# Order of the matmuls at the end of the output projection, and a PSUM value half copied out at the turn from up- to down-projection

## The chip, the cores and the metric

The kernel runs on one core of one Trainium2 chip. The metric is the device time of one execution in microseconds (us); lower is better. Three executions of the kernel before took 933.41, 936.21 and 936.86 us; their median, 936.21 us, is the number that the changed kernel is compared with.

## What is computed

One layer of a diffusion backbone for 512 latent tokens of width 1024, in float32. The last two parts matter here: the token mixer's output projection with its residual, and the feed-forward part with a 3x3 depthwise convolution (the tokens are an image of 8 rows and 64 columns).

```python
def _conv_ffn(h, rows, w_up, conv_w, conv_b, w_down):
    a, val = _split(h @ w_up, (D_FF, D_FF))                 # D_FF = 2816
    img = a.reshape(bsz, rows, length // rows, D_FF)
    a = conv3x3_depthwise(img, conv_w) + conv_b
    return (gelu(a) * val) @ w_down
...
x = x + g1x * (merged @ w_o)
hx2 = _modulate(_rms_norm(x, norm2_g), sh2x, sc2x)
x = x + g2x * _conv_ffn(hx2, rows, w_up, conv_w, conv_b, w_down)
return _rms_norm(x, final_norm_g)
```

## The kernel before

**Three matmuls for one.** Every float32 operand is split in a high part (rounded to the matmul's input type) and a low part (the rest). ScalarE (ACT) casts the high part, VectorE (DVE) subtracts to get the low part, and TensorE (PE) runs three matmuls: high by high, high by low, low by high. In the names, wh and wl are the parts of weights, h2h and h2l those of the normalised input of the feed-forward part, eh, el, sh, sl those of activations of the down-projection.

**Who sets the order.** The kernel is written with a tile framework: each engine's instructions are put in an order by the framework's scheduler from the written program, its own costs and the data dependencies, and every engine then runs its own list strictly in that order. The helper in_order (lines 81 to 90) chains all instructions of one engine from a given point, so that the scheduler keeps the written order there. DMA loads are issued from SyncE's queue (SP); some weight tiles get a second operand added by an accumulating DMA from GpSimd's queue (POOL).

**Output projection** (strassen, lines 445 to 494, called at 1494). The 512x1024 by 1024x1024 product is done in seven half-size products (Strassen-Winograd); each is 24 matmuls per pair of weight loads, done in two steps of 12 (j = 0, 1). Four PSUM banks of the pool "gl" and four of the pool "mm" hold the sums. The last product, s4, adds to the pair of gl banks c and completes the quarter for tokens 0 to 255. wo_done (1476 to 1487) is called for each finished 128x512 piece: DVE multiplies by the gate and adds to the residual x1, ACT squares for the norm. When a token row's two halves are there, norm2_tok makes its scale and the scaled tile xs on ACT. norm2_part (1453 to 1470) then transposes xs on PE into a gl bank, ACT turns each 128x256 piece into h2h and h2f (scale and shift), and DVE makes h2l. The tokens 256 to 511 are finished before s4 starts, so their transposes can be done while s4 runs: they stand in the list todo, whose entries are taken one at each step of the product (wo_step).

**Up-projection** (1530 to 1536, 1646 to 1658). It starts with four column blocks at once (prods_cm, line 388), whose matmuls for tokens 256 to 511 need h2h and h2l of one k after the other, k = 0 to 7. Then 20 more blocks f follow, each with two products of 24 matmuls into two mm banks: pa, which goes through the convolution, and pv, the value half. conv_part (1512 to 1528) copies pa out (ca), starts the accumulator (cacc) on ACT, adds eight taps on DVE (line 1523), applies gelu on ACT (1524), and multiplies by pv straight from its PSUM bank on DVE (1525). Every second block ends with four DVE sums, token_sums.

**Down-projection** (1538 to 1792). Again Strassen-Winograd, over 11 pairs p of hidden blocks. Units "x" (one p, 12 matmuls, banks p1 and p5, gl pool), "t3" and "t2" (two p each, 12 matmuls, banks p7 and p6, mm pool) alternate: x0, x1, t3, t2, x2, x3, t3, t2, and so on. prep(i) issues the work that unit i needs: for x (x_prep, 1572) an in-place add on the freshly loaded raw tile (line 1578, DVE), its split (ACT cast, DVE subtract, 1567 and 1568), splits of the activations (374, 375) and the sum t (1582, DVE); for t3 and t2 two half-tile splits. prep runs two units ahead of the matmuls (LEAD = 2). Weight pairs wh, wl rotate through five buffers, raw tiles through four.

At the turn, in the last up block f = 21, the first loads and the first two units are prepared, then conv_part for f = 21 is written, and then the loop over units starts. The mm pool has four banks: p7 takes two that are free, and the second p6 bank is the one in which pv of f = 21 lies.

## Time and profile before

| | |
|---|---|
| median of three executions | 936.21 us (933.41 to 936.86) |
| the profiled execution | 938.85 us, of which the span from first to last instruction is 937.1 us |
| mean granted TensorE clock | 0.990 |
| PE busy | 906.9 us, 97% of the span |
| DVE busy | 755.3 us, 81% |
| ACT busy | 484.2 us, 52% |
| HBM traffic | 142 GB/s over the span |

How to read the profile: times are us from the start of the span. A row of the timeline has the start, the duration, the engine, the line of the kernel, the operation, what it writes and reads, and in brackets how long the engine stood idle before it and what released it. Matmuls overlap, so the time that one costs is the distance between two starts, not the duration. A row of the windows view has the stretch, its length, then for each engine the busy time and the number of instructions, the granted TensorE clock (1.00 is full), the share of the DMA engines that is busy, and GB/s. The chain of waits is followed back from the last instruction: each row names what the end was waiting for at that time.

### The profile page before, as it was taken

The numbers are of one execution on the slowest core, as the hardware profiler recorded it, in microseconds if no ns is written. First come the engines' busy times: TensorE is split into PE (matmuls) and PEld (weight loads), VectorE is DVE, ScalarE is ACT, GpSimd is POOL, SyncE is SP. The second block draws the span as 40 slices with busy tenths as digits, with TensorE's granted clock in tenths as the row PEclk, the third lists the DMA queues.
The fourth block names the chain that finished last, engine by engine and source line by source line (L and its number), as shares of the span: only waits on it lengthen the run. The fifth ranks groups of instructions, "written<-read, shape, count | busy, mean of one in ns | idle before, by whom it ended". The sixth has DMA issues, their size and how long they took to land.

```text
span 937.1 us, 12863 instructions
## 1 busy us (share of the span) xinstructions
PE 906.9 (97%) x4671; PEld 758.9 (81%) x4671; DVE 755.3 (81%) x1312; ACT 484.2 (52%) x871; POOL 62.1 (7%) x90
## 2 busy tenths in 40 slices
PE   6999999999999999999999998999999999989996
PEld 4776898988888888878888877988888888868885
DVE  5567759689589877878776886999988898999797
ACT  5136546557465546656652569533333443356574
POOL 3000000000000011112011010000000000022100
PEclk9999999999999999999999999999999999989999
DMA  9941411141079375968677164344434333499432
GB/s 271 334 131 28 131 46 46 46 113 49 20 229 329 122 195 115 281 153 230 174 194 210 28 176 136 95 142 135 124 116 142 103 90 113 99 248 218 125 108 90
DMA packets 125820, 134.26 MB, mean 143 GB/s; under 512 B 7177, under 2 KB 84309, under 8 KB 125757
## 3 DMA queue, kind: packets, MB, share of 16 engines
q1 hardware_dynamic: 115357, 116.80, 40.1%
q0 software_dynamic: 8672, 15.43, 10.2%
q10 hardware_dynamic: 1728, 1.22, 0.4%
q8 instruction: 37, 0.61, 0.3%
q14 instruction: 26, 0.21, 0.1%
HBM read 131.32 MB, written 2.10 MB: 142 GB/s over the span
## 4 chain that ended last, share of the span: by engine, by line
PE 78%; DVE 10%; DMA 5%; ACT 3%; issue 2%; SPq 1%; ACTq 0%; DVEq 0%
PE mm L382 32%; PE mm L408 9%; PE gl L1625 6%; PE gl L455 5%; PE mm L1625 4%; PE gl L408 3%; PE mm L455 3%; PE gl L904 3%; PE mm L401 3%; DMA raw<-in_w_in_dram 2%; DVE wl L144 1%; PE mm L694 1%; PE mm L1008 1%; DVE bc L872 1%; PE mm L393 1%
## 5 line engine op out<-in xcount | busy, mean ns | idle before, releaser
L143 ACT CAST wh<-raw 128x1024 fp32r<-128x1024 f32 x110 | 115.0, 1049 | 89.0 <-PE mm L382 55.5
L144 DVE TENSOR_TENSOR wl<-raw,wh 128x1024 fp32r<-128x1024 f32 x110 | 133.9, 1220 | 31.3 <-ACT wh L143 30.9
L382 PE MATMUL mm<-h2l,wh 128*128 128x512 f32 (+1 forms) x352 | 133.7, 380 | 0.0
L382 PE MATMUL mm<-h2h,wl 128*128 128x512 f32 (+1 forms) x352 | 133.5, 379 | 0.0
L382 PE MATMUL mm<-h2h,wh 128*128 128x512 f32 (+1 forms) x352 | 133.5, 379 | 0.0
L1523 DVE SCALAR_TENSOR_TENSOR cacc<-ca,ccol,cacc 128x441 f32<-128x441 f32 (+2 forms) x176 | 121.7, 694 | 4.4 <-ACT cacc L1517 0.9
L382 PEld LDWEIGHTS mm<-h2l,wh 128*128 128x128 f32 x352 | 66.2, 188 | 12.6 <-DVE h2l L1470 0.2
L382 PEld LDWEIGHTS mm<-h2h,wl 128*128 128x128 f32 x352 | 66.2, 188 | 12.5
L382 PEld LDWEIGHTS mm<-h2h,wh 128*128 128x128 f32 x352 | 66.2, 188 | 12.5
L1524 ACT ACTIVATE cacc<-cacc 128x512 f32<-128x512 f32 x22 | 13.9, 633 | 91.9 <-DVE cacc L1523 91.9
L1157 DVE SCALAR_TENSOR_TENSOR acc<-wa,cs,acc 128x512 f32<-128x512 f32 x64 | 45.6, 747 | 4.2 <-DMA wa<-in_w_ada_dram 4.2
L382 PE MATMUL mm<-hxh,wh 128*128 128x512 f32 x104 | 41.7, 401 | 0.0
L382 PE MATMUL mm<-hxh,wl 128*128 128x512 f32 x104 | 40.9, 394 | 0.0
L382 PE MATMUL mm<-hxl,wh 128*128 128x512 f32 x104 | 40.7, 392 | 0.0
L218 DVE TENSOR_TENSOR wl<-tt,wh 128x512 fp32r<-128x512 f32 x48 | 31.7, 687 | 9.5 <-ACT wh L217 9.4
L217 ACT CAST wh<-tt 128x512 fp32r<-128x512 f32 x48 | 28.5, 622 | 19.9 <-DMA tt<-in_w_in_dram 7.5
L1567 ACT CAST wh<-raw 128x1024 fp32r<-128x1024 f32 x22 | 23.0, 1052 | 18.9 <-PE mm L1625 6.1
L193 POOL DMA_DIRECT2D tt<-in_w_in_dram x24 | 20.8, 1086 | 167.5 <-DVE xl L1258 72.1
L1568 DVE TENSOR_TENSOR wl<-raw,wh 128x1024 fp32r<-128x1024 f32 x22 | 26.9, 1222 | 4.4 <-ACT wh L1567 4.3
L455 PE MATMUL mm<-wl,hxh 128*128 128x512 f32 x72 | 28.1, 391 | 0.8 <-DVE wl L144 0.8
L455 PE MATMUL mm<-wh,hxh 128*128 128x512 f32 x72 | 28.1, 390 | 0.0
L455 PE MATMUL mm<-wh,hxl 128*128 128x512 f32 x72 | 28.0, 389 | 0.0
(522 smaller groups left out, 2397.5 us busy)
## 6 DMA issues: line engine op xcount, KB each, us to landing
raw<-in_w_in_dram SPq DMA_DIRECT2D x54, 512.0 KB, 4.7
wa<-in_w_ada_dram SPq DMA_DIRECT2D x96, 256.0 KB, 5.4
raw<-in_ffn_w_up_dram SPq DMA_DIRECT2D x44, 512.0 KB, 4.1
raw<-in_ffn_w_down_dram SPq DMA_DIRECT2D x22, 512.0 KB, 3.4
tt<-in_w_in_dram POOLq DMA_DIRECT2D x24, 256.0 KB, 6.7
raw<-in_w_br_a_dram SPq DMA_DIRECT2D x8, 512.0 KB, 5.3
raw<-in_w_br_b_dram SPq DMA_DIRECT2D x8, 512.0 KB, 4.4
raw<-in_w_o_dram SPq DMA_DIRECT2D x8, 512.0 KB, 5.9
```

The source lines that it names most:

```text
L143: A.copy(wh, raw)
L144: V.tensor_tensor(wl, raw, wh.bitcast(F32), op=ALU.subtract)
L217: A.copy(wh[:, kk, :], tt[j][kk])
L218: V.tensor_tensor(wl[:, kk, :], tt[j][kk], wh[:, kk, :].bitcast(F32), op=ALU.subtract)
L382: T.matmul(ps, a[:, k, :], b[:, c0:c0 + n], start=(k == 0 and i == 0), stop=(k == KT - 1 and i == 2))
L401: T.matmul(ps, a[:, t * P:(t + 1) * P], b[:, k % 4, :], start=(k == 0 and i == 0), stop=(k == KT - 1 and i == 2))
L408: T.matmul(ps, a, b[:, k % 2, :], start=(k == 0 and i == 0), stop=(k == KT - 1 and i == 2))
L455: T.matmul(ps[t], a, b[:, kk, :], start=(first and i == 0), stop=(j == 1 and kk == 1 and i == 2), skip_group_check=again)
L904: T.matmul(ps, p_, q_, start=(start and z == 0), stop=(stop and z == 2))
L1157: V.scalar_tensor_tensor(a_, w_, cs[:, k, 0:1], a_, op0=ALU.mult, op1=ALU.add)
L1523: V.scalar_tensor_tensor(o, a_[:, r0 + dy:r1 + dy, c0 + dx:c1 + dx], wcol(tap), o, op0=ALU.mult, op1=ALU.add)
L1625: T.matmul(ps, a[:, t * P:(t + 1) * P], w[b][:, j, c0:c0 + n], start=(first and i == 0), stop=(last and i == 2), skip_group_check=again)
```

## The change

The diff has two parts that don't touch each other.

1. In strassen, for the output projection only (low_first), all PE instructions from the product a12 (in c11) to the end of s4 are chained in written order. The transposes for tokens 256 to 511 move in the written program: instead of two pieces at the two steps of s4, all four come with the second step, after s4's last matmul (three idle entries in todo, then one entry for all).
2. conv_part becomes a generator, conv_steps. For the last block f = 21 its first piece runs where conv_part ran, and copies pv out of its bank into an SBUF tile pvc on ACT. The eight taps follow in pairs, one pair after each of the first down units, and gelu, the product with pvc and the token sums after the fourth pair.

```diff
+        start = len(traced())
         if low_first:
             c11()
         prod(c, "s4", True)
+        if low_first:
+            in_order(start, T.engine)
...
-                todo.extend([idle, idle, lambda: norm2_parts(1, (0, 1)), lambda: norm2_parts(1, (2, 3))])
+                todo.extend([idle] * 3 + [lambda: norm2_parts(1, range(4))])
...
-    def conv_part(f, pa, pv):
+    def conv_steps(f, pa, pv, keep=False):
         wcol = lambda tap: ccol[:, tap * FT + f:tap * FT + f + 1]
         a_ = heap([P, 8, GW], s="ca")
         A.copy(a_, pa)
         acc = heap([P, 8, GW], s="cacc")
         A.activation(acc, pa, AF.Identity, bias=ccol[:, 198 + f:199 + f], scale=wcol(4))
-        for tap in (0, 1, 2, 3, 5, 6, 7, 8):
+        gact.append(acc)
+        if keep:
+            pv_ = heap([P, 512], s="pvc")
+            A.copy(pv_, pv)
+            pv = pv_
+        yield
+        for n_, tap in enumerate((0, 1, 2, 3, 5, 6, 7, 8)):
...
+            if n_ % 2:
+                yield
         A.activation(acc, acc, AF.Gelu)
         V.tensor_tensor(acc, acc, pv.rearrange("p (r w) -> p r w", w=GW), op=ALU.mult)
-        gact.append(acc)
         if f % 2:
             token_sums(f // 2)
+
+    def conv_part(f, pa, pv):
+        for _ in conv_steps(f, pa, pv):
+            pass
...
-        conv_part(f, pa, pv)
+            last_conv = conv_steps(f, pa, pv, True)
+            next(last_conv)
+        else:
+            conv_part(f, pa, pv)
...
     for i in range(NX - 3):
         prep(i + LEAD)
+        next(last_conv, None)
         steps_x(i)
```

How the scheduler's lists change. First PE at the end of the output projection, before. gl_5604 and gl_5605 are the banks c of s4; wh_5720 and wl_5721 are the weights of its second step; rows that read ident are transposes, and xs_5703 and xs_5716 are scaled token tiles.

```order
L455 MATMUL gl_5605<-wh_5676,ml_5415 128x512
L1459 MATMUL gl_5782<-ident,xs_5703 128x128
L1459 MATMUL gl_5794<-ident,xs_5703 128x128
L455 MATMUL gl_5604<-wh_5720,mh_5354 128x512
L1459 MATMUL gl_5782<-ident,xs_5716 128x128
L1459 MATMUL gl_5782<-ident,xs_5703 128x128
L1459 MATMUL gl_5782<-ident,xs_5716 128x128
L1459 MATMUL gl_5794<-ident,xs_5716 128x128
L1459 MATMUL gl_5794<-ident,xs_5703 128x128
L1459 MATMUL gl_5794<-ident,xs_5716 128x128
L455 MATMUL gl_5604<-wl_5721,mh_5354 128x512
L455 MATMUL gl_5604<-wh_5720,ml_5355 128x512
```

The same place of the changed kernel, the end of s4 (line 1462 is the old 1459).

```order
L455 MATMUL gl_5605<-wh_5720,mh_5414 128x512
L455 MATMUL gl_5605<-wl_5721,mh_5414 128x512
L455 MATMUL gl_5605<-wh_5720,ml_5415 128x512
L1462 MATMUL gl_5800<-ident,xs_5703 128x128
L1462 MATMUL gl_5800<-ident,xs_5716 128x128
L1462 MATMUL gl_5812<-ident,xs_5703 128x128
```

Eight transposes stood ahead of eleven of s4's last twelve matmuls; now all twelve come first and the sixteen transposes follow in one row, ahead of every matmul of the up-projection. On ACT and DVE the instructions for s4's result (gate, residual, square) and one weight split move ahead of the first h2h, h2f and h2l.

Second, PE in down's first units, before. mm_7858 and mm_7859 are the two p6 banks, gl_7852 and gl_7853 the p1 banks, in which unit x2 starts with wh_7902.

```order
L1625 MATMUL mm_7858<-wh_7878,sl_7827 128x512
L1625 MATMUL gl_7852<-wh_7902,eh_7907 128x512
L1625 MATMUL gl_7852<-wl_7903,eh_7907 128x512
L1625 MATMUL gl_7852<-wh_7902,el_7908 128x512
L1625 MATMUL gl_7853<-wh_7902,eh_7907 128x512
L1625 MATMUL mm_7859<-wh_7878,sh_7806 128x512
L1625 MATMUL mm_7859<-wl_7879,sh_7806 128x512
```

And now (mm_7844 and mm_7845 are the p6 banks, gl_7838 is p1, line 1639 is the old 1625).

```order
L1639 MATMUL mm_7844<-wh_7866,sl_7807 128x512
L1639 MATMUL mm_7845<-wh_7866,sh_7806 128x512
L1639 MATMUL mm_7845<-wl_7867,sh_7806 128x512
L1639 MATMUL mm_7845<-wh_7866,sl_7807 128x512
L1639 MATMUL mm_7844<-wh_7866,sh_7826 128x512
```

The matmuls into the second p6 bank, six of which stood behind four of unit x2, now come in written order, right behind the first p6 bank.

Third, DVE in the same units, before. cacc_7833 is the accumulator of block 21; raw_7814 is the tile of unit x4, wl_7903 the low weights of x2.

```order
L1568 TENSOR_TENSOR wl_7879<-t_1506_7816,wh_7878 128x512
L1523 SCALAR_TENSOR_TENSOR cacc_7833<-ca_7831,ccol,cacc_7833 128x448
L375 TENSOR_TENSOR el_7908<-cacc_6401,eh_7907 128x512
L1523 SCALAR_TENSOR_TENSOR cacc_7833<-ca_7831,ccol,cacc_7833 128x7x63
L1568 TENSOR_TENSOR wl_7903<-raw_7789,wh_7902 128x1024
L1523 SCALAR_TENSOR_TENSOR cacc_7833<-ca_7831,ccol,cacc_7833 128x8x63
L375 TENSOR_TENSOR sl_7912<-s_1306_6492,sh_7911 128x512
```

And now.

```order
L1582 TENSOR_TENSOR wl_7867<-t_1506_7816,wh_7866 128x512
L1532 SCALAR_TENSOR_TENSOR cacc_7833<-ca_7831,ccol,cacc_7833 128x448
L1592 TENSOR_TENSOR raw_7814<-raw_7814 128x512
L1532 SCALAR_TENSOR_TENSOR cacc_7833<-ca_7831,ccol,cacc_7833 128x7x63
L1582 TENSOR_TENSOR wl_7893<-raw_7789,wh_7892 128x1024
L1532 SCALAR_TENSOR_TENSOR cacc_7833<-ca_7831,ccol,cacc_7833 128x8x63
L375 TENSOR_TENSOR el_7898<-cacc_6401,eh_7897 128x512
```

The in-place add on raw_7814 (line 1592, the old 1578) moves from behind the whole convolution to ahead of six of its taps and of the low weights of x2. The last tap, the product with pvc and the token sums move down by a few rows. On ACT the new copy stands behind the cast of x2's weights. On SP the load of the raw tile of unit x5 moves ahead of the load of b_1528 (the b tile of x4); nothing moves on POOL.

## Prediction

> **What bounds the kernel now.** I read the page's chain first, then the chain of waits in order of time, which names the few places where something other than PE sets the end.

> ```profile
> span 937.1 us, 12863 instructions
> ...
> PE 78%; DVE 10%; DMA 5%; ACT 3%; issue 2%; SPq 1%; ACTq 0%; DVEq 0%
> ```

> ```profile
> 565.79 1.86 ACT xs L1448 x3
> ...
> 577.07 5.90 PE mm L393 x47
> ...
> 830.89 0.61 DVE cacc L1525
> ```

> PE carries 78% of the chain: what the change wins or loses is what it does to PE's gaps. Both touched places are gaps: at 566 us PE hangs on the scaled tiles xs, at 831 us on the product with pv (line 1525). The timeline of PE around the first:

> ```profile
> 563.51 0.39 PE L455 MATMUL gl<-wh,ml 128*128 128x512 f32 x1
> 566.46 0.44 PE L1459 MATMUL gl<-ident,xs 128*128 128x128 f32 x2 [2.56 <-ACT xs L1448]
> ...
> 567.69 1.54 PE L1459 MATMUL gl<-ident,xs 128*128 128x128 f32 x6 [0.55 <-ACT xs L1448]
> ...
> 572.39 0.60 PE L1459 MATMUL gl<-ident,xs 128*128 128x128 f32 x4
> ```

> And around the second:

> ```profile
> 827.51 0.39 PE L1625 MATMUL gl<-wh,el 128*128 128x512 f32 x1
> 827.74 0.39 PE L1625 MATMUL gl<-wh,eh 128*128 128x512 f32 x1
> 831.63 0.76 PE L1625 MATMUL mm<-wh,sh 128*128 128x512 f32 x1 [3.51 <-DVE cacc L1525]
> ...
> 836.46 0.63 PE L1625 MATMUL gl<-wh,sh 128*128 128x512 f32 x1
> 836.89 0.45 PE L1625 MATMUL gl<-wl,sh 128*128 128x512 f32 x1
> ```

> Each gap has a second cost, seen in the windows view (PE's busy time and count, then DVE, ACT, POOL, the granted clock last but two):

> ```profile
> 563.90:567.40 3.50, 0.68 (x4) 0.36 (x3) 3.50 (x7) 3.49 (x7) 0.00 (x0) 0.99 0.93 270
> 567.40:570.80 3.40, 3.11 (x11) 2.73 (x12) 1.13 (x2) 3.40 (x9) 0.00 (x0) 0.51 0.92 267
> 826.80:830.20 3.40, 1.33 (x6) 0.75 (x4) 3.40 (x5) 2.08 (x4) 0.74 (x1) 1.00 1.11 271
> 830.20:833.60 3.40, 1.97 (x5) 1.61 (x6) 3.40 (x8) 1.86 (x4) 0.76 (x2) 0.50 1.00 234
> 833.60:837.00 3.40, 3.40 (x10) 2.63 (x9) 3.40 (x8) 0.99 (x1) 1.92 (x3) 0.50 0.84 273
> ```

> A stretch of 3.4 us in which PE worked little (0.68 or 1.33 us) is followed by one at half clock; one with 1.97 us of work by another half one; 3.11 and 3.40 us bring the clock back.

> **Part 1, the turn at the down-projection.** A warm matmul costs 827.74 - 827.51 = 0.23 us. After the one at 827.74 the next could start at 827.97; it starts at 831.63: 3.66 us idle. The twelve that start from 831.63 to 836.46 take until 836.89, 5.26 us instead of 12 x 0.23 = 2.7: another 2.5 us by the half clock. Removed: 6.2 us. With pv copied out, the second p6 bank is free when the copy ends, and the new order uses it behind three matmuls into the first.

> The copy is one ACT instruction more, priced by the like copy of pa:

> ```profile
> L1515 ACT COPY ca<-mm 128x512 f32<-128x512 f32 x22 | 12.7, 575 | 0.0
> ```

> ```profile
> 820.44 1.05 ACT L1567 CAST wh<-raw 128x1024 fp32r<-128x1024 f32 x1
> ```

> 0.58 us, right behind this cast of x2's weights, so it ends at about 822. The bank is needed six matmuls ahead of 827.74, at 826.4: some 4 us cover it. Without that cover it would cost PE its 0.58 us.

> What is late next is DVE, with PE 6 us earlier. Its row has no real gap here:

> ```profile
> 819.28 0.67 DVE L1523 SCALAR_TENSOR_TENSOR cacc<-ca,ccol,cacc 128x441 f32<-128x441 f32 x1
> ...
> 833.95 1.29 DVE L1568 TENSOR_TENSOR wl<-t,wh 128x512 fp32r<-128x512 f32 x2
> 835.15 0.69 DVE L1578 TENSOR_TENSOR raw<-raw 128x512 f32<-128x512 f32 x1
> ```

> From 819.28 to 835.15 it does the last taps, block 21's product and sums, and all that x2, x3, t3 and t2 need: 15.9 us. The new list does the same in another order, with the in-place add for x4 (0.6 us, half of the 1.20 from 833.95 to 835.15) drawn up behind two of the taps, to about 821.3. That add waits for its load, and everything on DVE is queued behind it. The load:

> ```profile
> raw<-in_ffn_w_down_dram SPq DMA_DIRECT2D x22, 512.0 KB, 3.4
> ```

> ```profile
> b<-in_ffn_w_down_dram POOLq DMA_DIRECT2D x2, 256.0 KB, 7.5
> ```

> ```profile
> 816.72 0.41 SPq L1550 DMA_DIRECT2D raw<-in_ffn_w_down_dram  x1
> ```

> Issued at 816.7, it lands between 820.1 (3.4, the median of all such loads) and 824.2 (7.5, the accumulating loads of this stretch). The DMA engines are full here, so I take 822.2, nearer the slow row: DVE waits 1.0 us and has the old work done at 835.15 + 0.6 + 1.0 = 836.8. Then come x4's low weights and x5's: a full split (1.13), four half tiles at 0.6, another split, and x5's el at 0.6: x4's weights at 837.9, x5's at 841.5, its el at 842.1.

> PE without a gap does a unit of 12 matmuls in 2.72 us. The first starts at 817.54 (827.74 less 45 matmuls), so x4, behind eight units, starts at 839.3 and x5 at 842.0; x5 wants its el three matmuls in, at 842.5. DVE is ahead by 1.5 us at x4 and by 0.3 to 0.4 at x5, and then gains: a group of four units is 9.5 us on DVE (two times 3.5, four times 0.6) against 10.9 on PE. I charge 0.3 us for a margin that small. Bounds of the charge: 0 and 2.0 (the load at 824.2 instead of 822.2). On SP the load for x5 now goes ahead of x4's b tile, which thus starts about 2.5 us later; x4's sum needs it near 840, so I cost it at nothing. Part 1: -6.2 + 0.3 = -5.9, from -6.2 to -4.2.

> **Part 2, the end of the output projection.** The eleven delayed matmuls now run at once: s4 ends at about 566.5. But the transposes still wait for xs, whose ACT list is unchanged up to there; the second of the pair is ready at 567.65 (the chain: 565.79 + 1.86). So the gap isn't removed: it moves behind s4, where the next work is the chain transposes, h2h, h2f, h2l. ACT and DVE there:

> ```profile
> 568.77 0.61 ACT L1480 ACTIVATE yt<-x 128x512 f32<-128x512 f32 x1
> 569.38 0.55 ACT L1466 ACTIVATE h2h<-gl,col_sh,am 128x256 fp32r<-128x256 f32 x1
> 569.84 0.55 ACT L1467 ACTIVATE h2f<-gl,col_sh,am 128x256 f32<-128x256 f32 x1
> 570.28 1.04 ACT L143 CAST wh<-raw 128x1024 fp32r<-128x1024 f32 x1
> 571.22 0.57 ACT L1466 ACTIVATE h2h<-gl,col_sh,am 128x256 fp32r<-128x256 f32 x1
> ...
> 575.34 0.28 ACT L498 ACTIVATE rstd<-n2s,eps_t 128x1 f32<-128x1 f32 x1
> ```

> ```profile
> 571.19 0.69 DVE L1478 TENSOR_TENSOR yt<-gl,g 128x512 f32<-128x512 f32 x1 [2.67 <-PE gl L455]
> ...
> 573.34 1.22 DVE L144 TENSOR_TENSOR wl<-raw,wh 128x1024 fp32r<-128x1024 f32 x1
> 574.47 0.42 DVE L1470 TENSOR_TENSOR h2l<-h2f,h2h 128x256 fp32r<-128x256 f32 x1
> ```

> From 569.38 ACT's new list has first a cast (0.94 between starts) and a square (0.61), then h2h (0.46) and h2f for k = 0, a cast, then k = 1, a root of about 0.25 and a square, then k = 2. DVE's 2.67 us wait is gone, so s4's result is not late. That gives for k = 0 h2h at 571.5 and h2l at 572.4; for k = 1 573.4 and, behind a residual add and a 1.13 us weight split, 574.55; for k = 2 575.15 and 576.05. A PE matmul here is 5.90/47 = 0.126 us, four with h2h and eight that need h2l. PE: k = 0 done at 573.4, k = 1 at 575.55, k = 2 at 577.05, k = 3 at 578.6. Before, the row at 577.07 is the first of k = 2's eight; with k = 3's twelve that is 577.07 + 20 x 0.126 = 579.6. So of the 5.2 us that PE lost here (572.39 - 563.74 less 12 x 0.23 and 8 x 0.09) only 1.0 us comes back.

> From that the clock takes its share: the stretch from 567.4 to 570.8 now holds transposes alone, well under 2 us, so by the windows above the next 3.4 us run at half clock. PE waits between k's there anyway: k = 0 ends at 574.3 instead of 573.4, and k = 3 at 578.75, 0.15 us of the gain. A second half-clock stretch would cost k = 1 too and make it 580.5, 0.9 us later than before. Part 2: -0.85, from -1.0 to +0.9.

> [...]

> The second half (tokens 0 to 255) follows on ACT about 0.7 us earlier, as PE does, so no new wait there.

> **Sum.** -5.9 - 0.85 = -6.75 us on the profiled execution's 938.85: 932.1, a ratio of 0.9928. On the median 936.21 that is 929.5. About 0.5% (4.7 us, 931.5) is what a measurement of this kernel can tell from no change.

> **Rivals.**
> - *The clock stays low at the output projection* for two stretches, part 2 +0.9: 936.21 - 5.0 = 931.2. For it: 1.97 us of work at half clock didn't bring it back. Against: there PE would be busy nearly all of the stretch.
> - *DVE holds PE up mildly*: the load lands at 824.2, PE loses 1.7 more at x5: -5.0, again 931.2. For it: full DMA engines. Against: nothing but the median.
> - *The gaps were longer under the profiler*: the profiled execution is 2.6 us above the median. If half-clock stretches cost others one window less, 2.5 is 1.2: 936.21 - 5.4 = 930.8; if all 2.6 us were such waits, 932.1.
> - *Slower: DVE becomes the bound.* The add is at the head of DVE's list, so a load later than 822.5 is paid in full by PE, and a PE gap over about 2 us also brings back the 2.5 us of half clock. Break-even is a delay of 4.3 us (4.3 + 2.5 = 6.8), a load landing at 826.8, ten us after its issue. At 831 it is 8.5 + 2.5 - 6.75: 940.5. The slowest row here, 7.5, speaks against.
> - *The bank isn't freed earlier* because the copy waits on ACT: part 2 alone, 935.4. The cast ahead of it has its tile long loaded; I see no cause.

> **Chances.** Forecast (928 to 931.4) 0.60, low clock 0.09, DVE mildly late 0.13, profiler 0.10, no effect 0.03, slower 0.05. Faster by over 0.5%: 0.56 of the first, most of the second and third (0.12), a little of the fourth: 0.70. Slower 0.05; the rest, 0.25, within. Range: below, all of both parts and no charge, 7.2 us, and the half-percent scatter of the runs: 927.0; above, both mild rivals together, 3.3 us: 933.5.

> **What would show it.** Right: no PE gap over 1 us between 818 and 845 and the clock at 1.00 there; the copy of pv on ACT before 824; DVE idle about 1 us ahead of line 1592; at the output projection a gap of about 1 us behind s4, then short waits on h2h and h2l, and k = 4 about 1 us earlier. Wrong: PE waiting for el or wl at x4 or x5 by several us, or half clock past 578.

## The result, and the profile after

The changed kernel took 930.77 us (median of seven executions, 928.0 to 934.33); the kernel before, run beside it, took 936.55 us (seven, 933.18 to 937.91). The ratio is 0.9947, with an interval from 0.9922 to 0.9972. By the ratio that is 5.0 us (2.6 to 7.3), where 6.75 were forecast.

The profiled execution of the changed kernel took 928.0 us. Its span, and what ends last on its chain:

```profile
span 926.3 us, 12858 instructions
...
PE 87%; DVE 5%; ACT 2%; DMA 2%; SPq 1%; issue 1%; DVEq 0%; ACTq 0%; POOLq 0%
```

The chain of waits from up's last block to the end of the down-projection, where line 1525 stood in it before:

```profile
813.17 5.44 PE gl L1639 x24
818.61 5.44 PE mm L1639 x24
824.05 5.44 PE gl L1639 x24
829.49 5.44 PE mm L1639 x24
...
913.81 3.64 PE mm L1639 x18
```

Not a single row of another engine: from the first matmul of the down-projection to its last PE waits for nothing. Between these two starts lie 105.11 us (813.01 to 918.12); before it was 111.41 (817.54 to 928.95). The turn gave 6.30 us in this pair of traces.

ACT, DVE and SyncE at the turn:

```profile
815.43 1.05 ACT L1581 CAST wh<-raw 128x1024 fp32r<-128x1024 f32 x1
816.38 0.58 ACT L1524 COPY pvc<-mm 128x512 f32<-128x512 f32 x1
```

```profile
816.17 0.68 DVE L1532 SCALAR_TENSOR_TENSOR cacc<-ca,ccol,cacc 128x448 f32<-128x448 f32 x1
816.76 0.68 DVE L1592 TENSOR_TENSOR raw<-raw 128x512 f32<-128x512 f32 x1
...
828.12 0.68 DVE L1536 TENSOR_TENSOR cacc<-cacc,pvc 128x512 f32<-128x512 f32 x1
...
836.00 0.69 DVE L375 TENSOR_TENSOR el<-cacc,eh 128x512 fp32r<-128x512 f32 x1
```

```profile
812.23 3.00 SPq L1564 DMA_DIRECT2D raw<-in_ffn_w_down_dram  x2
```

The copy ends at 816.96 and frees the bank 4.9 us before PE wants it (39 matmuls of 0.227 behind 813.01: 821.9). The product with pvc starts at 828.12, 15.1 us behind the first down matmul where it was 13.3 before, and nobody waits for it. The in-place add at 816.76 has no idle time before it: its load, the first of the two in the last row, issued at 812.23, was there within 4.5 us. Unit x5's el is written by 836.69; PE wants it at 813.01 + 110 x 0.227 = 838.0 (two behind the start of x5), 1.3 us later.

PE at the end of the output projection:

```profile
564.12 0.39 PE L455 MATMUL gl<-wh,ml 128*128 128x512 f32 x1
564.36 1.10 PE L1462 MATMUL gl<-ident,xs 128*128 128x128 f32 x8
565.97 0.66 PE L1462 MATMUL gl<-ident,xs 128*128 128x128 f32 x4 [0.52 <-DVE yt L1481]
567.29 0.66 PE L1462 MATMUL gl<-ident,xs 128*128 128x128 f32 x4 [0.67 <-DVE yt L1481]
568.32 0.74 PE L393 MATMUL mm<-h2h,wh 128*128 128x256 f32 x4 [0.37 <-ACT h2h L1469]
569.23 0.38 PE L393 MATMUL mm<-h2l,wh 128*128 128x256 f32 x1 [0.17 <-DVE h2l L1473]
...
571.30 0.39 PE L393 MATMUL mm<-h2l,wh 128*128 128x256 f32 x1 [0.39 <-DVE h2l L1473]
```

In this trace the wait for xs is gone; five short waits behind s4 stand in its place, 2.1 us together, two of them for DVE to empty the banks of s4. In the five other traces of this order (e2, e6, e9, e11 and e12 below) PE still waits 0.4 to 0.9 us for xs, now behind s4; in e2:

```profile
566.87 0.98 PE L1462 MATMUL gl<-ident,xs 128*128 128x128 f32 x7 [0.53 <-ACT xs L1451]
```

In the trace of the changed kernel the clock was full from 9.3 to 920.6 us. From the start of s4 to k = 4 it is 16.37 us (558.91 to 575.28) against 18.55 before (561.02 to 579.57): 2.2 us.

The two spans differ by 10.8 us: 6.3 and 2.2 at the two places, 0.2 in the up-projection, and 2.1 ahead of s4; that part had come up by 420 us, ahead of anything that was changed (over the fourteen traces shown or used here, s4 starts between 558.1 and 562.5 us). So one pair of traces says 8.5 for the change, and the seven executions of each say 5.0. Which is right, and what is each part worth?

### The profile page after: what moved, and what is told of

The parts are those of the page before. It is cut to its first block, busy times and chain, and to the rows that moved or that the text cites. A ratio compares the mean times of both kernels' runs of the same rounds, so it can differ in the third digit from the quotient of the medians.

```text
span 926.3 us, 12858 instructions
## 1 busy us (share of the span) xinstructions
PE 900.1 (97%) x4671; PEld 754.7 (81%) x4671; DVE 755.5 (82%) x1312; ACT 483.8 (52%) x872; POOL 61.9 (7%) x90
## 3 DMA queue, kind: packets, MB, share of 16 engines
q10 hardware_dynamic: 1728, 1.22, 0.4%
## 4 chain that ended last, share of the span: by engine, by line
PE 87%; DVE 5%; ACT 2%; DMA 2%; SPq 1%; issue 1%; DVEq 0%; ACTq 0%; POOLq 0%
PE mm L382 32%; PE mm L408 9%; PE gl L455 9%; PE mm L455 7%; PE gl L1639 6%; PE mm L1639 5%; PE gl L408 4%; PE gl L907 3%; PE mm L401 3%; PE mm L697 1%; PE mm L1011 1%; PE mm L393 1%; DVE bc L875 1%; SPq L319 1%; PE gl L938 1%
## 5 line engine op out<-in xcount | busy, mean ns | idle before, releaser
L143 ACT CAST wh<-raw 128x1024 fp32r<-128x1024 f32 x110 | 115.1, 1049 | 89.6 <-PE mm L382 56.5
L144 DVE TENSOR_TENSOR wl<-raw,wh 128x1024 fp32r<-128x1024 f32 x110 | 133.7, 1218 | 30.3 <-ACT wh L143 28.1
L1581 ACT CAST wh<-raw 128x1024 fp32r<-128x1024 f32 x22 | 23.0, 1052 | 17.6 <-PE mm L1639 8.5
L455 PE MATMUL mm<-wl,hxh 128*128 128x512 f32 x72 | 28.1, 391 | 0.0
L455 PE MATMUL mm<-wh,hxh 128*128 128x512 f32 x72 | 28.0, 389 | 0.0
L455 PE MATMUL mm<-wh,hxl 128*128 128x512 f32 x72 | 28.0, 389 | 0.0
## 6 DMA issues: line engine op xcount, KB each, us to landing
raw<-in_w_in_dram SPq DMA_DIRECT2D x54, 512.0 KB, 4.7
wa<-in_w_ada_dram SPq DMA_DIRECT2D x96, 256.0 KB, 5.1
raw<-in_ffn_w_up_dram SPq DMA_DIRECT2D x44, 512.0 KB, 4.2
raw<-in_ffn_w_down_dram SPq DMA_DIRECT2D x22, 512.0 KB, 3.5
tt<-in_w_in_dram POOLq DMA_DIRECT2D x24, 256.0 KB, 6.7
raw<-in_w_br_a_dram SPq DMA_DIRECT2D x8, 512.0 KB, 4.9
raw<-in_w_br_b_dram SPq DMA_DIRECT2D x8, 512.0 KB, 4.2
raw<-in_w_o_dram SPq DMA_DIRECT2D x8, 512.0 KB, 5.7
```

Source lines behind the costliest of these rows:

```text
L143: A.copy(wh, raw)
L144: V.tensor_tensor(wl, raw, wh.bitcast(F32), op=ALU.subtract)
L455: T.matmul(ps[t], a, b[:, kk, :], start=(first and i == 0), stop=(j == 1 and kk == 1 and i == 2), skip_group_check=again)
```

## The experiments

Theory: the turn is worth PE's idle time plus the half clock behind it, and the output projection 1 to 2 us. Rivals: the turn is worth less than its profile shows; most of the gain is the output projection's; the spread of the taps is what helps; DVE becomes the bound. All ratios are to the kernel before, run on the same chip beside them.

**The turn alone** (e1): the changed kernel with the output projection as before.

```diff
-        if low_first:
-            in_order(start, T.engine)
...
-                todo.extend([idle] * 3 + [lambda: norm2_parts(1, range(4))])
+                todo.extend([idle, idle, lambda: norm2_parts(1, (0, 1)), lambda: norm2_parts(1, (2, 3))])
```

> Only the second part of the change: pv of block 21 copied out, its taps spread; the output projection as before. Theory (the freed bank is worth 3.7 us of idle time and 2.5 us of half clock, the output projection's end 1 to 2 us more): 5 to 6.5 us under the kernel before, ratio 0.9930 to 0.9947, and no PE gap over 1 us between up's last block and unit x6. Rival (the unprofiled executions lose only one half-clock window at the turn, so the turn is worth 3.5 to 4.5 us): ratio 0.9952 to 0.9963. Rival (most of the 5.8 us measured is the output projection's): ratio over 0.9968.

Measured: 0.9958 (0.9943 to 0.9973), 3.9 us. The trace has no gap, 105.11 us again. The 6.2 of the profile is too much; the first rival's number holds.

**The output projection alone** (e2): the kernel before with the chain on PE and the transposes moved.

```diff
         if low_first:
             c11()
         prod(c, "s4", True)
+        if low_first:
+            in_order(start, T.engine)
...
-                todo.extend([idle, idle, lambda: norm2_parts(1, (0, 1)), lambda: norm2_parts(1, (2, 3))])
+                todo.extend([idle] * 3 + [lambda: norm2_parts(1, range(4))])
```

> Only the first part of the change: PE tied into written order from a12 to the end of s4, all transposes behind it; the turn as before. Theory by the recorded sum: 0.85 us under the kernel before, ratio 0.9991; by the changed kernel's profile 2.1 us, ratio 0.9978; the half clock at the turn is still there. Rival (the order only moves the gap behind s4 and costs a half-clock stretch): ratio 0.9995 to 1.0010, with half clock behind s4 in the profile. Rival (it carries most of the gain): ratio under 0.9965.

Measured: 0.9996 (0.9979 to 1.0013). By timing alone 0.85 can't be told from 0, and 2.1 lies just outside the interval. But its trace shows the old turn a second time. PE there, and the windows view of two stretches of 3.41 us: the one that holds most of that wait, and the next:

```profile
828.16 0.47 PE L1628 MATMUL mm<-wh,sh 128*128 128x512 f32 x1 [2.16 <-DVE cacc L1528]
```

```profile
826.10:829.51 3.41, 1.35 (x6) 1.17 (x7) 3.41 (x8) 2.28 (x4) 0.93 (x2) 1.00 1.10 270
829.51:832.93 3.42, 3.42 (x10) 2.65 (x9) 3.42 (x9) 0.40 (x1) 1.71 (x3) 0.50 0.77 240
```

The same wait is 2.16 us here where it was 3.51, and one stretch follows at half clock, not two. The turn takes 109.14 us: 4.03 over the gapless 105.11, not 6.30. The instructions and their order are the same; so what differs is something that varies from execution to execution.

**Copy without spread** (e3) and **spread without copy** (e4), both with the old output projection:

```diff
-            next(last_conv)
+            for _ in last_conv:
+                pass
```

> Output projection as before; pv of block 21 is copied out, but its taps, gelu, product and sums are written at once, as before. Theory (the bank is all that mattered, and DVE has the slack): the same as the turn alone within 0.5 us, ratio 0.9930 to 0.9950, PE without a gap at the second p6 bank. Rival (the spread is needed, because taps in front of the low weights of the first units hold PE up once the bank doesn't): PE waits 1 to 3 us for el or wl of x2 to x5, and at least 2 us of the turn's gain is missing, ratio over 0.9952.

```diff
-            last_conv = conv_steps(f, pa, pv, True)
+            last_conv = conv_steps(f, pa, pv)
```

> Output projection as before; the taps of block 21 are spread behind the first units, but its product still reads pv from the PSUM bank. Theory: no gain, since the bank is freed no earlier; the product stands two places later on DVE (0.6 to 1.2 us), against which PE has five more matmuls ahead of the wait (1.1 us): ratio 0.9990 to 1.0015, with the gap of 3 to 4 us and the half clock still there. Rival (the spread takes load off DVE and so the product comes earlier): ratio 0.9950 to 0.9985.

Measured: the copy alone 0.9959 (0.9940 to 0.9977) with a turn of 105.11 us, the spread alone 0.9995 (0.9975 to 1.0014). The spread is worth nothing; the copy is all. PE in the spread alone:

```profile
832.97 0.76 PE L1636 MATMUL mm<-wh,sh 128*128 128x512 f32 x1 [4.15 <-DVE cacc L1533]
```

Here the wait is 4.15 us, and longer than the list explains (the product is 1.2 us later on DVE, and five more matmuls, 1.1 us, run ahead of the wait). These traces give what varies. DVE's waits during the up-projection (590 to 818 us; the line, what it waited for, us in total, times, longest) in the kernel before, in e2 and in e4:

```profile
DVE raw L1578 <- DMA raw<-in_ffn_w_down_dram: 1.9, 2, 1.2
DVE acc L1157 <- DMA wa<-in_w_ada_dram: 0.2, 1, 0.2
```

```profile
DVE raw L1581 <- DMA raw<-in_ffn_w_down_dram: 0.9, 1, 0.9
```

```profile
DVE acc L1157 <- DMA wa<-in_w_ada_dram: 1.9, 1, 1.9
DVE raw L1589 <- DMA raw<-in_ffn_w_down_dram: 0.7, 1, 0.7
```

What DVE waited for a load in the up-projection it didn't make good before the turn, but for some 0.3 to 0.5 us. Its lag at the turn (start of block 21's first tap, less start of the first down matmul) follows from these waits, and PE's idle time from the lag:

| trace | DVE's waits for loads | lag | idle at the bank | half-clock stretches | turn |
|---|---|---|---|---|---|
| before | 2.1 | 1.74 | 3.66 | 2 | 111.41 |
| e2 | 0.9 | 0.38 | 2.31 | 1 | 109.14 |
| e4 | 2.6 | 2.31 | 4.32 | 2 | 111.76 |
| after | 2.3 | 1.78 | 0 | 0 | 105.11 |
| e1 | 1.0 | 0.56 | 0 | 0 | 105.11 |
| e3 | 1.3 | 0.80 | 0 | 0 | 105.11 |

The lag is the waits less 0.3 to 0.5 us (less 0.4 to 0.6 in e7 to e10 and e12 below), the idle time of the old order is the lag plus 1.92 (e4's 4.32 is 2.31 + 1.92 + 1.2 - 1.1), and with the copy a lag of 0.56 to 1.78 costs nothing. The next two experiments make the lag by hand.

**DVE later, before and after** (e5, e6): four in-place maxima on block 20's accumulator, 2.4 us.

```diff
+        if f == FT - 2:
+            for _ in range(4):
+                V.tensor_tensor(acc, acc, acc, op=ALU.max)
         A.activation(acc, acc, AF.Gelu)
```

> The kernel before, with four more DVE instructions in block 20 (in-place maxima of the accumulator with itself, 0.6 us each, which change no value): DVE comes to the turn 2.4 us later. Theory (PE's gap at the second p6 bank is 1.8 us plus DVE's lag, and DVE makes nothing of a lag good before the turn): a gap of 4.6 to 6.6 us there, 2.4 us longer than with the same loads before, half clock behind it, and 2 to 3.5 us over the kernel before, ratio 1.002 to 1.004. Rival (the gap is set by something other than DVE's queue): gap and time unchanged.

> The changed kernel with the same four DVE instructions in block 20 (2.4 us). Theory (with the bank freed DVE has a margin of about 1.4 us at unit x5 in an execution whose lag is 1.8 us, and more in one with less lag): PE waits 0 to 1.0 us for x5's activations, no half clock, 0 to 1 us over the changed kernel, ratio to the kernel before 0.9945 to 0.9965. Rival (DVE is the bound at the turn and every us added is paid): PE waits 2.4 us or more at x4 or x5, ratio over 0.9975.

In the old order the lag became 3.26 (waits 1.3 - 0.4 + 2.4), but the scheduler, which saw the longer list, drew seven more of x2's matmuls (1.6 us) ahead of the wait:

```profile
828.98 0.39 PE L1628 MATMUL gl<-wl,sh 128*128 128x512 f32 x1
832.62 0.47 PE L1628 MATMUL mm<-wh,sh 128*128 128x512 f32 x1 [3.25 <-DVE cacc L1528]
```

Idle 3.41 us, 0.2 under lag + 1.92 - 1.6, and one half-clock stretch: a turn of 110.21. The gap of 4.6 us or more didn't come, because of those seven matmuls. The time, 1.0008 (0.9981 to 1.0034), is 1.1 us under the low end expected; its interval holds no effect as well as most of the range expected. In the changed kernel the lag became 2.98:

```profile
837.33 0.50 PE L1642 MATMUL gl<-wl,eh 128*128 128x512 f32 x1 [0.20 <-DVE wl L1585]
```

That is the first PE wait of the new turn, ahead of the second matmul of x4 (the 98th of the down-projection), for x4's low weights and not, as expected, for x5's activations; the turn is 105.62, 0.51 longer. The scheduler had redrawn DVE's list: the in-place add for x4, which the changed kernel has ahead of six taps (816.76), stands behind the token sums again (833.66); x4's low weights are done 22.3 us behind the first down matmul, where it is 19.5 in the changed kernel. The time, 0.9970 (0.9953 to 0.9987), ends just above the range expected, but its interval reaches well into it.

**The wait filled** (e7): the kernel before, with ten matmuls by a tile of zeros in PE's wait, PE chained there.

```diff
...
+            for _ in range(10):
+                T.matmul(bank["p1"][1], zr, w4[0][:, 0, :], start=False, stop=False)
...
+            in_order(start, T.engine)
...
```

> The kernel before, with ten matmuls by a tile of zeros into unit x2's second p1 bank, between the four matmuls of x2 and the first one into the second p6 bank; they add nothing to the sums and fill about 2.3 us of PE's wait. Theory (half clock follows a 3.4 us stretch in which PE worked too little, and costs about 1 us in the mean over executions beside 3 us of idle time): the product with pv is as late as before, PE's wait shrinks to 0 to 2 us, no half clock at the turn, and 0.5 to 2.5 us under the kernel before, ratio 0.9973 to 0.9995. Rival (the whole loss is idle time and the half clock is nothing): ratio 0.9997 to 1.0010. Rival (half clock is nearly the whole loss): ratio under 0.9965.

```profile
825.73 2.49 PE L1742 MATMUL gl<-wh,zr 128*128 128x512 f32 x10
828.24 0.47 PE L1628 MATMUL mm<-wh,sh 128*128 128x512 f32 x1
```

The lag was 0.59; PE gets on no sooner, but the clock stays full, and the turn is 107.75 us. Against e2's 109.14 at a lag of 0.38 that is 1.4 us, 1.6 for equal lags: one half-clock stretch. Measured: 0.9991 (0.9973 to 1.0009), as expected, though the interval holds no effect, too. The mean granted clock rose from 0.9927 to 0.9948.

**ACT chained, too** (e8):

```diff
-            in_order(start, T.engine)
+            in_order(start, T.engine, A.engine)
```

> The changed kernel with ACT, too, tied into written order from a12 to the end of s4, so that all h2h and h2f of tokens 256 to 511 stand ahead of two weight casts and of the square and root of s4's result. Theory (the 2.1 us that PE still waits behind s4 are waits on ACT's and DVE's lists): waits on h2h and h2l shrink by 0.5 to 1 us, k = 4 starts up to 1 us earlier, ratio to the kernel before 0.993 to 0.9955. Rival (the banks of s4 set the pace, and the second half of the tokens, now behind, is late): no gain, or PE waits 0.5 to 2 us at the transposes of tokens 0 to 255, ratio 0.9955 to 0.9975.

```profile
571.05 1.23 PE L393 MATMUL mm<-h2h,wh 128*128 128x256 f32 x4 [3.60 <-ACT h2h L1469]
```

```profile
567.61 2.92 ACT L143 CAST wh<-raw 128x1024 fp32r<-128x1024 f32 x3
570.44 0.56 ACT L1469 ACTIVATE h2h<-gl,col_sh,am 128x256 fp32r<-128x256 f32 x1
```

A miss: 0.9972 (0.9953 to 0.9991). In the list that came out, three weight casts stand in a row ahead of the first h2h (in the changed kernel it is one, the other two ran ahead of xs); PE waited 3.60 us for it, with a half-clock stretch behind, and s4's start to k = 4 took 18.23 us. Neither theory had that wait.

**Move without chain** (e9), the changed kernel less the call of in_order, and **chain without move** (e10), the changed kernel with todo as before:

```diff
-        if low_first:
-            in_order(start, T.engine)
```

> The changed kernel without the chain on PE: only the transposes of tokens 256 to 511 stand behind s4 in the written program. On every engine this gives the changed kernel's order, row for row, so the chain is worth nothing by itself and this is a second sample of the changed kernel: ratio to the kernel before 0.9930 to 0.9965, half clock neither at the turn nor for more than one stretch at the output projection. A ratio over 0.997 would say that the gain first measured was in good part scatter.

```diff
-                todo.extend([idle] * 3 + [lambda: norm2_parts(1, range(4))])
+                todo.extend([idle, idle, lambda: norm2_parts(1, (0, 1)), lambda: norm2_parts(1, (2, 3))])
```

> The changed kernel with the transposes written where they were (two pieces at two steps of s4), PE chained in that order: eight transposes stand ahead of the whole second step of s4. Theory (what counts is what stands behind the wait for xs): PE waits 2.5 to 3.2 us for xs inside s4 as in the kernel before, and then runs s4's twelve matmuls in one piece; k = 4 starts 0 to 1 us later than in the changed kernel without half clock, 1.5 to 3 us with it; ratio to the kernel before 0.994 to 0.997. Rival (the chain is what helps): same as the changed kernel in the trace.

e9: 0.9950 (0.9930 to 0.9969). It is the changed kernel's order on every engine, so the chain on PE does nothing that the move of the transposes doesn't do. e10: 0.9968 (0.9950 to 0.9985). PE's two waits for xs, inside s4:

```profile
563.02 0.33 PE L1462 MATMUL gl<-ident,xs 128*128 128x128 f32 x1 [2.00 <-ACT xs L1451]
564.25 0.98 PE L1462 MATMUL gl<-ident,xs 128*128 128x128 f32 x7 [0.90 <-ACT xs L1451]
```

From s4's start to k = 4 it takes 18.32 us, one half-clock stretch among them, against 17.02 in e9. By the traces, what counts is what stands behind the wait; in timing the intervals of e9 and e10 overlap.

**DVE much later** (e11): as e6, with nine maxima.

```diff
+        if f == FT - 2:
+            for _ in range(9):
+                V.tensor_tensor(acc, acc, acc, op=ALU.max)
         A.activation(acc, acc, AF.Gelu)
```

> The changed kernel with nine in-place maxima in block 20 (5.4 us of DVE, no value changed). Theory (DVE has a margin of 1.5 to 2.5 us at x4 and x5 and PE pays what goes beyond it): PE waits 2.5 to 4.5 us for x4's low weights, with one or two half-clock stretches behind it, 4 to 7 us over the changed kernel, ratio to the kernel before 0.998 to 1.003: the whole gain of the turn is gone. Rival (DVE can make the lag good behind the turn): PE waits under 1 us, ratio under 0.9965.

```profile
PE gl L1642 <- DVE wl L1585: 1.6, 2, 1.0
PE mm L1642 <- DVE wl L1585: 0.2, 1, 0.2
PE mm L1642 <- DVE cacc L1539: 0.2, 1, 0.2
```

Measured: 0.9989 (0.9974 to 1.0004); the turn is 108.99 us, 3.88 longer, at a lag of 4.78. (Two of the maxima and block 20's product run behind block 21's first tap here, so the lag shows too little; by the waits it is 1.4 - 0.4 + 5.4 = 6.4.) The gain is gone, as expected, but otherwise than expected: no single long wait at x4, but four waits of 0.2 to 1.0 us and shorter delays beside them, spread over 17 us (824.4 to 841.2) from the second p6 bank to x4, and the clock stays full there. Here, too, the add for x4 stands behind the token sums (837.50).

**The changed kernel without the spread** (e12): e3's edit on the changed kernel.

> The changed kernel without the spread of the taps: pv is copied out, and taps, gelu, product and sums of block 21 are written at once. Theory (the copy alone carries the turn): the same as the changed kernel, the turn without a PE gap, ratio to the kernel before 0.9930 to 0.9965. Rival (the spread is needed once the output projection is faster, too): PE gap over 0.5 us between x2 and x6, ratio over 0.9970.

Measured: 0.9954 (0.9935 to 0.9972), turn 105.11 us. The spread isn't needed.

## Why the prediction was right, and where it was too large

**Removed at the turn: 6.2 us (3.66 idle, 2.5 half clock).** Right for the execution it was read from (6.30 in the pair of traces), too large for the others: timed, the turn gives 3.9 (e1, 2.5 to 5.3) and 3.8 us (e3, 2.2 to 5.6). This is the term that was mis-sized. The idle time: over the eleven traces without added DVE work the lag is 0.32 to 2.31 us, 1.15 in the mean; the lag plus 1.92 is about 3.1 us, not 3.66. The half clock: the mean granted clock of 28 executions of the kernel before is 0.9932, that of e1 and e3 0.9943 and 0.9944, a difference of 0.0011 of 934 us, or 1.0 us; 3.1 and 1.0 make 4.1, near the 3.9 that was measured. But e7, which removes the half clock at the turn and leaves the wait, raised the mean clock by 0.0021, 2.0 us, and all four traces in which PE stands idle at the bank (before, e2, e4, e5) have one or two half-clock stretches there, 1.7 us or more (an estimate: half of each 3.41); 3.1 and 2.0 make 5.1, inside both intervals. So the half clock costs some 1 to 2 us in the mean, and how the excess divides between idle time and half clock stays open. The profiled execution had a long lag and two half-clock stretches; the prediction saw that it was 2.6 us above the median, and scaled it by 0.9928 instead of asking which of its waits made it long.

**The copy on ACT is covered (4 us).** It is, by 4.9.

**DVE waits 1.0 us for x4's load, charge 0.3.** It didn't wait at all: the load came within 4.5 us of its issue, sooner than the 5.5 (822.2 less 816.7) that was taken between the median row (3.4) and the accumulating one (7.5). Without that wait the forecast margin of 0.3 to 0.4 us at x5 becomes 1.3 to 1.4; in the trace it is 1.3. The charge should have been nothing; the sums for x4 and x5 were right but for that wait.

**The slower rival, DVE as the bound.** It exists: nothing is lost at a lag of 1.78, 0.51 us with 2.4 us of DVE work added (e6, at x4) and 3.88 with 5.4 added (e11, from the second p6 bank to x4). Those two kernels have another list on DVE, so the changed kernel's own edge isn't measured. What made DVE late was not only the load of x4 but every load that it waited for in the up-projection (0.9 to 2.6 us in all in the table above).

**The output projection: the gap moves behind s4, 1.0 of 5.2 us comes back.** The mechanism is right: short waits behind s4, as forecast. For the size, from s4's start to k = 4:

| | traces, us |
|---|---|
| old order | 18.55, 19.49, 17.30, 19.57, 18.27, 17.97 (before, e1, e3, e4, e5, e7) |
| new order | 16.37, 17.06, 17.18, 17.02, 16.99, 17.62 (after, e2, e6, e9, e11, e12) |

18.5 against 17.0 in the mean: 1.5 us; the forecast had k = 4 at 578.6, 17.6 behind the start of s4. The one old trace without half clock is e3, 17.30: by that one trace the order itself gives some 0.3 us, and the rest goes with the half clock, which the old order had in five of six traces and the new one in one of six (e11).

**The clock's share there: 0.15 lost.** This step failed in sign. The forecast took "well under 2 us" of transposes to be too little; the stretches behind s4 have 1.8 to 2.25 us of work, and five of six kept the clock. It was the old order whose stretches fell short (0.67 us from 563.94 to 567.35 in the kernel before). In timing the part stays small: e2 says 0.4 us (-1.2 to 2.0), and the changed order in three samples (0.9947, 0.9950, 0.9954) against the turn alone in two (0.9958, 0.9959) 0.4 to 1.1, with intervals that overlap. Whether it is 1.5, 0.4 or nothing stays open.

**The sum.** -5.9 - 0.85 was forecast; 3.9 for the turn and 0.4 to 1.1 for the output projection are measured, 4.3 to 5.0. The rival "the gaps were longer under the profiler" had the number, 930.8, but not the cause: a profiled execution can have short gaps, as e2's shows, and of the thirteen kernels other than the one before (the changed one, e1 to e12) nine had a profiled execution faster than their median. The upper end of the range isn't the sum that it names: 929.5 + 3.3 is 932.8, not 933.5.

## What to carry to other kernels

PE's wait for DVE, which didn't catch up, grew with DVE's lag here (2.31 us at a lag of 0.38, 3.66 at 1.74), and the lag was the sum of its waits for loads less some 0.5 us; before you price such a wait from one trace, add those up and ask what they are in other executions. Free the bank with a copy on an engine that has time (0.58 us on ACT, for the 3.8 us of e3), and check the margin that the late engine has left: here 1.3 us in the changed kernel's trace, while 2.4 us more of its work cost 0.5 us and 5.4 us more cost 3.9. Work that can't start yet belongs behind work that can, in the written order (s4's start to k = 4 took 17.02 us in e9 and 18.32 in e10); tying PE's list on top of that did nothing, and tying ACT's brought a new wait (3.60 us in e8).

## What the runs showed of the hardware

```profile
561.99:565.40 3.41, 1.48 (x10) 1.25 (x11) 3.10 (x7) 3.41 (x8) 0.00 (x0) 1.00 1.10 297
565.40:568.81 3.41, 3.41 (x10) 2.63 (x9) 1.24 (x3) 3.38 (x8) 0.00 (x0) 0.50 0.74 195
```

```profile
561.15:564.57 3.42, 1.51 (x7) 0.93 (x5) 3.42 (x9) 3.39 (x6) 0.00 (x0) 1.00 0.53 156
564.57:567.98 3.41, 2.12 (x13) 1.68 (x14) 2.80 (x4) 3.41 (x8) 0.00 (x0) 1.00 1.01 278
```

The way back took more: 1.36 to 2.87 us of work at half clock left it there (e1's row below), 3.02 us and over brought it back.

```profile
563.95:567.36 3.41, 2.87 (x10) 2.28 (x11) 2.50 (x4) 3.41 (x9) 0.00 (x0) 0.50 1.10 288
567.36:570.78 3.42, 3.42 (x10) 2.64 (x8) 1.47 (x3) 2.79 (x6) 0.00 (x0) 0.50 0.51 145
```

What the same gap cost went by where it fell in these stretches: e3 and e1 have the same wait for xs (2.64 and 2.69 us), which e3's boundary at 564.57 cuts into 1.9 and 0.7 us, and e1's at 563.95 into 2.3 and 0.4. e3 kept its clock, e1 lost it for two stretches, and from s4's start to k = 4 they took 17.30 and 19.49 us. The stretches don't begin with this work: in the old order the half clock begins 6.33 us behind the start of s4 in the kernel before (567.35) and 5.15 us behind it in e1 (563.95).
